# Eight key staging buffers, later scratch stores, new modelled costs and emission times, and another place for one FFN, in a two-layer decoder trunk on eight cores

## Chip, cores, metric

The kernel runs on the eight NeuronCores of one Trainium2 chip, one batch element on each. The metric is device microseconds of the slowest core. Cores 0 to 3 are one die, 4 to 7 the other. In some executions one die or both run at a lower granted clock and the time grows by some per cent; such runs are called slow, and only fast runs, or the cores of a die that was not disturbed, are compared here. On the chips of the experiments slow runs were frequent, so beside the ratios I give the *clean-die time*: for every die whose cores had a granted clock of 0.965 or more (median of its four cores), the span of its slowest core; of these values over all executions the median.

## The reference, cut

```python
D_MODEL, BATCH, SEQ, D_FF = 1024, 8, 4096, 2816
for i in range(2):                                 # layer 0: GLA, layer 1: differential attention
    x = x + 0.5 * swiglu_ffn(rms_norm(x, g), w_in, w_down)
    x = x + mixers[i](rms_norm(x, mix_norms[i]))
    x = x + 0.5 * swiglu_ffn(rms_norm(x, g2), w_in2, w_down2)
return rms_norm(x, final_norm)
# GLA: chunked gated linear attention, 4 heads, a state carried from chunk to chunk
# differential attention: 8 heads, causal; out = (softmax(Q1 K1') - lambda * softmax(Q2 K2')) V
```

## The kernel before

A core walks through its 4096 tokens in eight tiles of 512. For each tile `u` there are tasks: `gu0`/`down0` (first FFN), `gproj` (GLA projections), `core` (the sequential GLA chain), `gout`, `gu1`/`down1`, `gu2`/`down2` (two FFNs), `dproj` (Q, K, V of the differential attention), `att`, `dout`, `gu3`/`down3` (last FFN, final norm; it also stores the tile and loads the tokens of tile `u + 2`).

The program is a straight list of instructions for each engine, written by a small scheduler when the kernel is built. The scheduler keeps a *modelled* time of every engine and tile. It emits, of all pieces that are ready in modelled time, the one with the lowest key; each task has a range of keys from `v0` to `v1`. The modelled costs therefore do nothing on the chip except fix the order of instructions on each engine and queue. What is emitted early or late stays so in the list.

```python
    def _cost(self, eng, ins):                          # modelled duration, modelled latency
        ...                                             # PE: columns / 2400, + 0.1 for a row switch
            return c, 0.15
        if eng is self.act:
            return 0.2 + n * 0.0008, 0.1
        if eng is self.dve:
            return 0.15 + n * 0.00105, 0.1
        return (0.25 + n * 0.0012 if n > 16 else 0.3 + n * 0.1), 0.1
    def dma(self, q, dst, src, pairs, size=65536):
        ...
        self.dma_free = max(self.dma_free, at) + size / 235e3     # one modelled pipe for all queues
        done = max(at + 2.5, self.dma_free + 1.5)
```

Weights come in slots of up to 512 KB in a ring of twelve. On first use a slot is read as float32 and cast on the way by a DMA of the POOL queue (`wpack`; page of before: 160 of 512 KB, in the median 27.0 us from issue to landing), stored as bfloat16 to a scratch in HBM (`wscr`; 160, 12.4 us), and on later uses reloaded from there by the SP queue (1120, 4.4 us). A reload into a ring place must wait for the scratch store from that place; on core 3 the SP queue waited 185.4 us in all for scratch stores.

```python
    def acquire(sid):
        ...
        if t_scr[sid] is None:
            t_scr[sid] = Tl(f"scr{sid}", wst_sem[i])
            k.dma(SP, t_scr[sid], t_wring[i], [(wscr[sid, :, 0:ln], wring[i][:, 0:ln])], 256 * ln)
        return i
```

The keys of a tile are copied from PSUM by VectorE into one of two staging buffers and stored to HBM (`kvc`); the attention loads keys and values back in blocks.

```python
        def k_cons(c, b):                                # c: one of eight key chunks, b: its PSUM bank
            i = c % 2
            def chain():
                yield Need(DVE, rd=[t_bank[b]], wr=[t_kst[i]], cond=lambda: kdone[i])
                kdone[i] = False
                k.op(DVE, lambda: nc.vector.tensor_copy(out=kst[i][:], in_=bank[b][:]), ...)
                putbank(b)
                yield Need(SP, rd=[t_kst[i]])
                k.dma(SP, t_kc[c, t], t_kst[i], [(kvc[c, t, :, 0:512], kst[i][:])], 131072)
                kdone[i] = True
            spawn(chain())
```

The softmax here doesn't subtract the row's maximum and nothing guards it: scores larger than these inputs give would overflow.

## Time and profile before

| | before |
|---|---|
| time, median of 3 runs | 6155.62 us (6155.39 to 6157.76) |
| span of the profiled execution | 6197.9 us (core 6); core 3 6154.1 us |
| PE busy, VectorE, ScalarE | 92%, 41%, 34% |
| idle of PE in gaps over 0.8 us, core 3 | 363 us, 194 of them before 1000 us |

The gaps are mine: the start of each matmul record minus the start of the one before and its streaming time as the kernel's model has it (2400 columns per us, 4800 for matmuls of 64 rows; the trace of before, core 3, shows 512 columns every 0.216 us, and two 64-row matmuls of 256 columns, started 4 ns apart, every 0.110 us). The model's 0.1 us for a row switch is in keeping: at 5800.1 us four such 64-row matmuls take 0.32 us to the first start of the 128-row matmuls behind them, where two times 0.110 make 0.22. Where I name the task of a matmul, I matched the records one for one with the scheduler's list; cores 0 and 6 miss some records, so I read core 3. Core 6 also had one stretch of 160.8 us at a granted clock of 0.8125 (cores 0, 1 and 7 had one too), core 3 none; at that clock it costs about 30 of the 44 us between their spans, an estimate.

From the page of before, the engine line of PE (busy us, share of the span, instructions) and the line of the chain that ended last:

```profile
PE 5712.1 (92%) x36586; PEld 2907.6 (47%) x37216; DVE 2512.6 (41%) x4435; ACT 2120.1 (34%) x3826; POOL 530.9 (9%) x1070
...
PE 79%; DMA 9%; DVE 5%; issue 3%; ACT 2%; POOL 1%; SPq 1%; DVEq 0%; ACTq 0%; POOLq 0%
```

PE bounds the kernel; a gain comes from PE's idle time. The table of waits of before, core 6 (who waited for whom: us in total, times, longest). L1246 is the key copy, L732 and L880 are matmuls of the next tasks:

```profile
DVE sb_work L1246 <- DMA kvc<-sb_work: 137.6, 28, 37.3
...
PE ps_all L732 <- DVE sb_work L1246: 51.3, 7, 11.3
...
PE ps_all L880 <- DVE sb_work L1246: 44.4, 1, 44.4
```

The copy waits for the store of an older chunk, holds its PSUM bank meanwhile, and PE runs out of banks. I call such a wait of PE a stand. Two such places in the timeline of before, core 3, PE alone (start us, us, engine, line, operation, in brackets the idle time before and what ended it): the first key projection, and the seventh.

```profile
764.47 1.89 PE L880 MATMUL ps_all<-sb_wring,sb_hT 128*128 128x512 bf16 x8
810.65 1.87 PE L880 MATMUL ps_all<-sb_wring,sb_hT 128*128 128x512 bf16 x4 [44.28 <-DVE sb_work L1246]
...
4947.43 1.89 PE L732 MATMUL ps_all<-sb_hT,sb_wring 128*128 128x512 bf16 x8 [0.62 <-DVE sb_hT L629]
4959.84 2.72 PE L732 MATMUL ps_all<-sb_hT,sb_wring 128*128 128x512 bf16 x6 [10.53 <-DVE sb_work L1246]
```

The end of the kernel, core 3, cut into the stretch from `gout_7` to the start of attention 7, and attention 7 itself (busy time of each engine, granted clock, DMA share, GB/s):

```profile
5355.00:5722.00 367.00, 365.82 (x1830) 171.72 (x1830) 138.16 (x201) 67.60 (x133) 13.38 (x30) 1.00 0.49 154
5722.00:6001.00 279.00, 262.56 (x3134) 158.65 (x3134) 64.13 (x167) 245.95 (x324) 17.89 (x38) 0.99 0.54 153
```

In the first stretch PE is full; in the second it idles 16 us, and ScalarE (fourth busy time) is at 88%.

### The profile page before, as it was taken

The numbers are of one execution on the slowest core, as the hardware profiler recorded it, in microseconds if no ns is written. First come the engines' busy times: TensorE is split into PE (matmuls) and PEld (weight loads), VectorE is DVE, ScalarE is ACT, GpSimd is POOL, SyncE is SP. The second block draws the span as 40 slices with busy tenths as digits, with TensorE's granted clock in tenths as the row PEclk, the third lists the DMA queues.
The fourth block names the chain that finished last, engine by engine and source line by source line (L and its number), as shares of the span: only waits on it lengthen the run. The fifth ranks groups of instructions, "written<-read, shape, count | busy, mean of one in ns | idle before, by whom it ended". The sixth has DMA issues, their size and how long they took to land.

```text
span 6197.9 us, 103483 instructions; the slowest of 8 cores (6154.1 to 6197.9 us)
## 1 busy us (share of the span) xinstructions
PE 5712.1 (92%) x36586; PEld 2907.6 (47%) x37216; DVE 2512.6 (41%) x4435; ACT 2120.1 (34%) x3826; POOL 530.9 (9%) x1070
## 2 busy tenths in 40 slices
PE   5897759999999999999999999999999999899998
PEld 2443324444444454445544454445544445444554
DVE  3432155335633454334633345333453334443223
ACT  1211132124311452135411563115731157511791
POOL 1111111000100010010100001000010000100000
PEclk9998979999999999999999999998999999999999
DMA  9879967664345634465344753555534565345652
GB/s 217 200 172 210 207 145 183 189 195 147 123 139 168 185 129 140 149 188 155 126 141 149 202 151 120 157 165 160 151 120 142 170 181 158 91 159 147 172 152 99
DMA packets 331317, 984.58 MB, mean 159 GB/s; under 512 B 38447, under 2 KB 55232, under 8 KB 330816
## 3 DMA queue, kind: packets, MB, share of 16 engines
q1 hardware_dynamic: 306432, 891.88, 46.6%
q0 software_dynamic: 24384, 86.04, 9.5%
q8 instruction: 311, 5.10, 0.3%
q14 instruction: 190, 1.56, 0.1%
HBM read 944.11 MB, written 119.70 MB: 172 GB/s over the span
## 4 chain that ended last, share of the span: by engine, by line
PE 79%; DMA 9%; DVE 5%; issue 3%; ACT 2%; POOL 1%; SPq 1%; DVEq 0%; ACTq 0%; POOLq 0%
PE ps_all L732 36%; PE ps_all L807 17%; PE ps_all L1361 8%; PE ps_all L880 7%; PE ps_all L1326 4%; DMA sb_wring<-wpack 4%; PE ps_all L860 3%; DMA kvc<-sb_work 2%; PE ps_all L619 2%; DMA wscr<-sb_wring 2%; ACT sb_work L1331 1%; DMA sb_xt<-x 1%; DVE sb_hT L629 1%; DVE sb_work L1374 1%; SPq L222 1%
## 5 line engine op out<-in xcount | busy, mean ns | idle before, releaser
L732 PE MATMUL ps_all<-sb_hT,sb_wring 128*128 128x512 bf16 (+2 forms) x11344 | 2543.5, 376 | 110.7 <-DVE sb_work L1246 51.3
L732 PEld LDWEIGHTS ps_all<-sb_hT,sb_wring 128*128 128x128 bf16 x11648 | 1112.8, 99 | 1366.6 <-issue 192.7
L807 PE MATMUL ps_all<-sb_wring,sb_work 128*128 128x512 bf16 x5443 | 1289.4, 384 | 75.2 <-DMA sb_wring<-wpack 60.9
L1331 ACT ACTIVATE sb_work<-ps_all 128x1024 bf16<-128x1024 f32 (+1 forms) x1088 | 1019.5, 1000 | 389.8 <-PE ps_all L1326 387.3
L739 ACT ACTIVATE sb_th<-ps_all 128x512 f32<-128x512 f32 x704 | 420.2, 597 | 1923.1 <-PE ps_all L732 1913.8
L743 DVE SCALAR_TENSOR_TENSOR sb_tg<-sb_th,ps_all 128x512 f32<-128x512 f32 x704 | 483.4, 687 | 1147.8 <-ACT sb_th L739 1146.9
L807 PEld LDWEIGHTS ps_all<-sb_wring,sb_work 128*128 128x128 bf16 x5632 | 537.8, 98 | 693.7 <-issue 115.5
L880 PE MATMUL ps_all<-sb_wring,sb_hT 128*128 128x512 bf16 x2467 | 605.9, 387 | 79.3 <-DVE sb_work L1246 44.4
L600 ACT ACTIVATE sb_junk<-sb_xt 128x512 bf16<-128x512 f32 x448 | 282.0, 630 | 1082.0 <-DVE sb_xt L675 799.6
L1361 PE MATMUL ps_all<-sb_work 128*128 128x129 bf16 x8448 | 633.0, 222 | 12.5 <-DVE sb_work L1374 9.7
L751 DVE TENSOR_TENSOR sb_work<-ps_all,sb_tg 128x512 bf16<-128x512 f32 x704 | 486.4, 691 | 363.4 <-PE ps_all L732 317.5
L1361 PEld LDWEIGHTS ps_all<-sb_work 128*128 128x128 bf16 x8448 | 516.8, 98 | 195.6 <-issue 122.6
L675 DVE SCALAR_TENSOR_TENSOR sb_xt<-ps_all,sb_xt 128x512 f32<-128x512 f32 x256 | 172.7, 688 | 635.1 <-PE ps_all L807 616.9
L880 PEld LDWEIGHTS ps_all<-sb_wring,sb_hT 128*128 128x128 bf16 x2560 | 243.3, 99 | 349.8 <-issue 107.4
L1326 PE MATMUL ps_all<-sb_work 64*128 64x256 bf16 (+1 forms) x4352 | 356.5, 272 | 23.3 <-ACT sb_work L1331 18.3
L860 PE MATMUL ps_all<-sb_hT,sb_wring 128*128 128x512 bf16 x1492 | 349.1, 380 | 13.3 <-DVE sb_hT L629 7.4
L629 DVE TENSOR_TENSOR sb_hT<-ps_all,sb_norms 128x1024 bf16<-128x1024 bf16 x192 | 233.9, 1220 | 209.1 <-PE ps_all L619 198.2
L610 POOL TENSOR_SCALAR sb_ssq<-sb_ssq 128x1 f32<-128x1 f32 x224 | 87.0, 388 | 2685.6 <-ACT sb_junk L600 2685.0
L1326 PEld LDWEIGHTS ps_all<-sb_work 64*128 64x128 bf16 x4352 | 159.7, 95 | 227.0 <-issue 186.4
L860 PEld LDWEIGHTS ps_all<-sb_hT,sb_wring 128*128 128x128 bf16 x1536 | 146.6, 98 | 183.2 <-issue 21.4
L646 DVE TENSOR_SCALAR sb_hb<-sb_xt,sb_rstd 128x1024 bf16<-128x1024 f32 x192 | 143.9, 751 | 213.7 <-POOL sb_rstd L613 213.5
L619 PE MATMUL ps_all<-sb_ident,sb_hb 128*128 128x128 bf16 x1536 | 123.4, 227 | 80.2 <-DVE sb_hb L646 80.0
(87 smaller groups left out, 2478.6 us busy)
## 6 DMA issues: line engine op xcount, KB each, us to landing
sb_wring<-wscr SPq DMA_DIRECT2D x1120, 512.0 KB, 4.4
sb_work<-kvc SPq DMA_DIRECT2D x576, 258.0 KB, 3.0
sb_wring<-wpack POOLq DMA_DIRECT2D x160, 512.0 KB, 27.0
wscr<-sb_wring SPq DMA_DIRECT2D x160, 512.0 KB, 12.4
sb_xt<-x SPq DMA_DIRECT2D x32, 512.0 KB, 15.4
out<-sb_xt SPq DMA_DIRECT2D x32, 512.0 KB, 12.4
sb_wring<-wscr SPq DMA_DIRECT2D x56, 256.0 KB, 3.3
kvc<-sb_work SPq DMA_DIRECT2D x64, 130.0 KB, 15.0
```

The source lines that it names most:

```text
L600: k.op(ACT, lambda: nc.scalar.activation(out=junk[:], in_=xt[:, p, s, of * 512:(of + 1) * 512], func=AF.Square, accum_out=ssq[:, p, s, of: ...
L629: k.op(DVE, lambda: nc.vector.tensor_tensor(out=dst, in0=pt[:, :, :], in1=norms[:, n_idx, :].unsqueeze(2).to_broadcast([128, KC, 128]), op ...
L732: k.op(PE, lambda: nc.tensor.matmul(bank[b][:, lo:lo + n], lhsT=w[:, kc, u * 128:(u + 1) * 128], rhs=hT[:, p, kc, lo:lo + n], start=(kc == ...
L739: k.op(ACT, lambda: nc.scalar.activation(out=th[q][:], in_=bank[bg][:], func=AF.Tanh, scale=0.5), reads=[t_bank[bg]], writes=[t_th[q], t_b ...
L743: k.op(DVE, lambda: nc.vector.scalar_tensor_tensor(out=tg[r][:], in0=th[q][:], scalar=1.0, in1=bank[bg][:], op0=ALU.add, op1=ALU.mult), re ...
L751: k.op(DVE, lambda: nc.vector.tensor_tensor(out=act[:, c, :], in0=bank[bu][:], in1=tg[r][:], op=ALU.mult), reads=[t_tg[r], t_bank[bu]], wr ...
L807: k.op(PE, lambda: nc.tensor.matmul(bank[b][:], lhsT=act[:, c, s * 128:(s + 1) * 128], rhs=wring[i][:, (c % 4) * 512:(c % 4 + 1) * 512], s ...
L860: k.op(PE, lambda: nc.tensor.matmul(bank[b][:], lhsT=w[:, kc, cc * 128:(cc + 1) * 128], rhs=hT[:, p, kc, :], start=(kc == 0), stop=(kc == ...
L880: k.op(PE, lambda: nc.tensor.matmul(bank[b][:], lhsT=hT[:, p, kc, s * 128:(s + 1) * 128], rhs=wring[i][:, (kc % 4) * 512:(kc % 4 + 1) * 51 ...
L1326: k.op(PE, lambda: nc.tensor.matmul(psall[:, b0 + m, kk * 256:kk * 256 + w], lhsT=lhs, rhs=qT[m * 64:(m + 1) * 64, h, qs:qs + w], start=Tr ...
L1331: k.op(ACT, lambda: nc.scalar.activation(out=pT[pi][:, :, 0:ncol], in_=psall[:, b0:b0 + 2, 0:ncol], func=AF.Exp, scale=0.125), reads=[t_ba ...
L1361: k.op(PE, lambda: nc.tensor.matmul(obv[j][:, m, 0:129], lhsT=pT[pi][:, m, c0:c0 + 128], rhs=v, start=(it["first"] and kk == 0 and m == 0) ...
```

## The change

It means to take away the wait for the key staging, to bring the modelled durations nearer to the measured ones, to leave more work of the next tile for the end of each attention, and to give attention 7 (the last, with no next tile) tile 6's last FFN as company. Measured, core 3 of before, medians: a matmul of 512 columns took 0.38 us (its end as the profile models it) and ScalarE started 0.10 us later, 0.48 in all, modelled with its latency as 0.36 before and 0.46 after; ScalarE's squares took 0.63 us and the read of their sum 0.19, 0.82 together, modelled as 0.61 and 0.80; POOL's TENSOR_TENSOR of two columns took 0.71 us, modelled as 0.50 and 0.72; VectorE's operations on 512 columns took 0.69 us, modelled as 0.69 and 0.68. For the two DMA rates no measurement stands here: they are my estimates.

```diff
-        self.dma_free = 0.0
+        self.dma_free = {"sp": 0.0, "pool": 0.0}
...  # PE latency 0.15 -> 0.25; ACT, DVE, POOL latency 0.1 -> 0.2
-            return 0.2 + n * 0.0008, 0.1
+            return 0.2 + n * 0.0008 + (0.19 if len(ins.ins.outs) > 1 else 0.0), 0.2
-            return 0.15 + n * 0.00105, 0.1
-        return (0.25 + n * 0.0012 if n > 16 else 0.3 + n * 0.1), 0.1
+            return 0.22 + n * 0.0009, 0.2
+        if ins.ins.opcode == "TensorTensor":
+            return 0.41 + n * 0.157, 0.2
+        return 0.23 + n * 0.0012, 0.2
...
-        self.dma_free = max(self.dma_free, at) + size / 235e3
+        self.dma_free[q.name] = max(self.dma_free[q.name], at) + size / (180e3 if q.name == "pool" else 220e3)
...  # scratch store: no longer in acquire, but in a side chain, at the latest in release
+            keep[i] = sid
+            spawn(keeper(i, sid))
+    def keeper(i, sid):
+        yield Need(SP, rd=[t_wring[i]])
+        keep_now(i, sid)
...
-            i = c % 2                                    # key staging; value staging moves up by 6 KB
+            i = c                                        # eight buffers, kdone goes
...
-        v = (B + 0.0, B + 0.45, B + 0.7) if u != 1 else (-1.9, -1.7, -1.6)
+        v = (B + 0.0, B + 0.53, B + 0.79) if u != 1 else (-1.9, -1.7, -1.6)
...  # gproj: B + 0.7 to B + 1.06  ->  B + 0.79 to B + 1.14
-             ... B + 1.1, B + (3.2 if spare else 1.6), 76)              # gu3; spare: tile 6
+             ... B + (2.9 if spare else 1.1), B + (3.7 if spare else 1.6), 76)
-             B + (3.2 if spare else 1.6), B + (4.0 if spare else 2.6), 38)   # down3
+             B + (3.7 if spare else 1.6), B + (4.0 if spare else 2.6), 38)
```

More of the change, by code (lines that the diff above doesn't have):

```diff
@@ L164, in _cost @@
             eng.rows = rows
-            return c, 0.15
+            return c, 0.25
         if eng is self.act:
-            return 0.2 + n * 0.0008, 0.1
+            return 0.2 + n * 0.0008 + (0.19 if len(ins.ins.outs) > 1 else 0.0), 0.2
         if eng is self.dve:
-            return 0.15 + n * 0.00105, 0.1
-        return (0.25 + n * 0.0012 if n > 16 else 0.3 + n * 0.1), 0.1
+            return 0.22 + n * 0.0009, 0.2
+        if ins.ins.opcode == "TensorTensor":
+            return 0.41 + n * 0.157, 0.2
+        return 0.23 + n * 0.0012, 0.2
     def op(self, eng, fn, reads=(), writes=(), inc=True):
@@ L215, in dma @@
         q.free = at + 0.1 * len(pairs)
-        self.dma_free = max(self.dma_free, at) + size / 235e3
-        done = max(at + 2.5, self.dma_free + 1.5)
+        self.dma_free[q.name] = max(self.dma_free[q.name], at) + size / (180e3 if q.name == "pool" else 220e3)
+        done = max(at + 2.5, self.dma_free[q.name] + 1.5)
         for t in srcs:
@@ L442, in acquire, with keep_now @@
         if t_scr[sid] is None:
+            keep[i] = sid
+            spawn(keeper(i, sid))
+        return i
+    keep = {}
+    def keeper(i, sid):
+        yield Need(SP, rd=[t_wring[i]])
+        keep_now(i, sid)
+    def keep_now(i, sid):
+        if keep.get(i) == sid:
+            keep.pop(i)
             ln = slot_len(sid)
@@ L445, in acquire @@
             k.dma(SP, t_scr[sid], t_wring[i], [(wscr[sid, :, 0:ln], wring[i][:, 0:ln])], 256 * ln)
-        return i
     def release(i):
+        if i in keep:
+            keep_now(i, keep[i])
         rg["free"].append(i)
@@ L1189, in gla_core @@
         pool.update({4, 5})
-    kst_sem = [k.dsem(f"kst{i}") for i in range(2)]
+    kst_sem = [k.dsem(f"kst{i}") for i in range(8)]
     vst_sem = [[k.dsem(f"vst{i}_{h}") for h in range(4)] for i in range(2)]
@@ L1201, in diff_proj @@
         t_qT = [k.view(f"qT{h}", A_QT + h * TT * 2, A_QT + (h + 1) * TT * 2) for h in range(8)]
-        kst = [carve(R_ACT + i * 1024, 1024, BF16) for i in range(2)]
-        t_kst = [k.view(f"kst{i}", R_ACT + i * 1024, R_ACT + (i + 1) * 1024) for i in range(2)]
+        kst = [carve(R_ACT + i * 1024, 1024, BF16) for i in range(8)]
+        t_kst = [k.view(f"kst{i}", R_ACT + i * 1024, R_ACT + (i + 1) * 1024) for i in range(8)]
         VB = 4 * 4 * 130 * 2
-        vo = R_ACT + 2048
+        vo = R_ACT + 8192
         vst = [carve(vo + i * VB, VB, BF16, "p (h s c) -> p h s c", h=4, s=4) for i in range(2)]
@@ L1211, in diff_proj @@
         vleft = [NS, NS]
-        kdone = [True, True]
         def v_cons(hf, s, b):
@@ L1240, in k_cons @@
         def k_cons(c, b):
-            i = c % 2
+            i = c
             def chain():
-                yield Need(DVE, rd=[t_bank[b]], wr=[t_kst[i]], cond=lambda: kdone[i])
-                kdone[i] = False
+                yield Need(DVE, rd=[t_bank[b]], wr=[t_kst[i]])
                 k.op(DVE, lambda: nc.vector.tensor_copy(out=kst[i][:], in_=bank[b][:]),
@@ L1251, in chain @@
                 k.dma(SP, t_kc[c, t], t_kst[i], [(kvc[c, t, :, 0:512], kst[i][:])], 131072)
-                kdone[i] = True
             spawn(chain())
@@ L1460, in _build @@
         task(f"gproj_{u}", lambda u=u: gla_proj(u), [f"~down0_{u}"]
-             + ([f"dproj_{u - 1}"] if u else []), B + 0.7, B + 1.06, 43)
+             + ([f"dproj_{u - 1}"] if u else []), B + 0.79, B + 1.14, 43)
         task(f"core_{u}", lambda u=u: gla_core(u), [f"gproj_{u}"] + ([f"att_{u - 1}"] if u else []), -500.0, -500.0, 1)
@@ L1478, in _build @@
         task(f"gu3_{t}", lambda t=t, g=spare: ffn_gu(t, 3, G_E if g else A_KV),
-             [f"~dout_{t}", f"att_{t}"] + ([f"core_{t + 1}"] if spare else []), B + 1.1, B + (3.2 if spare else 1.6), 76)
+             [f"~dout_{t}", f"att_{t}"] + ([f"core_{t + 1}"] if spare else []), B + (2.9 if spare else 1.1), B + (3.7 if spare else 1.6), 76)
         task(f"down3_{t}", lambda t=t, g=spare: ffn_down(t, 3, final_block(t), not g), [f"~gu3_{t}"],
-             B + (3.2 if spare else 1.6), B + (4.0 if spare else 2.6), 38)
+             B + (3.7 if spare else 1.6), B + (4.0 if spare else 2.6), 38)
     for t in range(min(2, NTL)):
```

## The prediction

> **What bounds the kernel now.** TensorE: the page's engine table has PE busy 5712 of 6198 us (92%), VectorE 41%, ScalarE 34%; the chain that ended last is PE for 79%, DMA for 9%. A gain must come from time in which PE idles or runs at half clock. On core 3 (6154 us in the table of cores) the gaps over 0.8 us between matmul records sum to 363 us, 194 of them before 1000 us. From 372 to 744 us the slices show the DMA engines full (about 1.03); the change moves no fewer bytes, so this stays.
>
> **Eight key staging buffers.** With two, the copy of key chunk 2 waits until chunk 0's store landed, and holds its PSUM bank. The table of waits: VectorE at the key copy waits 137.6 us in 28 waits for the store; PE waits 51.3 + 44.4 us for the copy. On core 3 PE stands 44.5 us at 766 us, then 4.8, 4.9, 7.1, 9.8, 8.8 and 10.7 us after the next six key projections: about 90. A half-clock stretch (granted 0.5) follows each and outlasts the gap, costing about 2 us each. [...] In the last six places nearly all should come back: stores will be issued during the query projection, and landing takes 10 to 15 us here. At 766 us the SP queue is also held by slot stores and reloads (one per 5.5 us up to 802 us), so I count 30 of 44. Together 90 us.
>
> **Scratch stores as the slot lands.** Slightly later, in the same queue: about 0.
>
> **Recalibrated costs and times.** PE waits for transposes whose inputs are late: about 5 us in most cores of the linear attention, 1 to 3 us around it, 2.8 us in each key projection, because the order assumed shorter latencies. Longer ones put filler there, and the later emission times leave some 17 instead of 7 us of the next tile's projection for each attention's end. These places idle about 125 us; I count 42, because tile 7's core has little filler.
>
> **FFN of tile 6 beside attention 7.** Its 75 us of gate and up matmuls all ran before 5723 us, in a full stage. Attention 7 takes 286 us with 37 us of filler. Its steps take 0.915 us on PE (QK, PV, two row switches) against 0.904 us per exponential on ScalarE (timeline): both nearly full; filler adds its own length. Only the waits over 0.2 us, about 20 us with clock loss, are recovered: 12 us.
>
> **Sum.** 90 + 42 + 12 = 144 us, less 14 for new waits of a new order: 130 us.
>
> Predicted 6025 us, range 5975 to 6095. Chances: faster by over 2% (below 6032.5) 0.55, within 2% 0.43, slower 0.02.
>
> **Right if** PE's wait for the key copy falls under 10 us; the 766 us gap shrinks by over 25; the 5 us gap goes in most cores; attention 7's stage grows to about 330 us while the stage before shrinks by about 65; the slices from 372 to 744 us stay.
>
> **Wrong if** key stores land so late that the next FFN's activation writes, which reuse the staging space, or attention's key loads wait; the new order exposes waits where tile 6's FFN was filler; or the startup's DMA order shifts.

The sum came to 90 + 42 + 12 - 14 = 130 us.

## The result, and the profile after

| | before | after |
|---|---|---|
| median | 6155.51 us (6153.78 to 6157.76, 4 runs) | 6078.63 us (fast runs 6072.95 to 6081.79; one slow run 7032.02) |
| ratio of fast runs | | 0.9872, 95% interval 0.9852 to 0.9891 |
| idle of PE in gaps over 0.8 us, core 3 | 363 us (169 after 1000 us) | 271 us (109 after 1000 us) |
| PE busy | 92% | 95% |

A ratio is the mean time of one kernel's fast runs over that of the other's of the same rounds, so not quite the ratio of the medians quoted beside it. The gain is 77 us by the medians; I had predicted 130, with 6095 us as the upper end. The 77 us are probably low: in the profiled run of after, the cores of die 0 had some 30 stretches of at most 8 us at a granted clock of 0.8125 (170 us in all on core 3), those of die 1 none, and in all three fast runs die 1 was done sooner (slowest core 6057 to 6064 us, die 0 6072 to 6081). Against die 1 the gain is 91 us or more.

From the page of after, the same two lines:

```profile
PE 5741.2 (95%) x37536; PEld 2917.1 (48%) x37536; DVE 2509.4 (41%) x4435; ACT 2119.3 (35%) x3826; POOL 525.9 (9%) x1070
...
PE 85%; DMA 7%; DVE 3%; issue 2%; ACT 2%; POOL 1%; SPq 1%; DVEq 0%; POOLq 0%; ACTq 0%
```

The table of waits of after, core 2. The key copy is L1260 here; L1339 is the attention's QK matmul:

```profile
DVE sb_work L1260 <- PE ps_all L876: 128.3, 64, 10.0
...
PE ps_all L1339 <- DMA sb_work<-kvc: 23.0, 2, 21.5
```

The copy now waits for PE alone, and PE for the copy not at all. But PE waits 23 us for the first load of keys and values. The same two places as before, timeline of after, core 3, PE:

```profile
788.47 0.58 PE L977 MATMUL ps_all<-sb_wg2b,sb_work 17*128 17x512 bf16 x1 [9.62 <-ACT sb_work L1014]
809.03 0.50 PE L1339 MATMUL ps_all<-sb_work 64*128 64x256 bf16 x4 [19.98 <-DMA sb_work<-kvc]
...
4872.13 1.89 PE L876 MATMUL ps_all<-sb_hT,sb_wring 128*128 128x512 bf16 x8
4878.32 1.01 PE L635 MATMUL ps_all<-sb_ident,sb_hb 128*128 128x128 bf16 x8 [4.30 <-DVE sb_hb L662]
```

Both stands have been replaced by another. At the first place, 44 us became 9.6 and 20 us. Before the 9.6 us, ScalarE's exponentials of the linear attention (L1012, L1014) waited 11.5 us for a key store to land: their output `Eb` lies over the eight staging buffers. At the seventh projection, 10.5 us became 4.3 us, and this new stand, a wait for the transposes (L635) of the next tokens' norm, is there after all six later projections with the same length; in the kernel before these transposes never caused more than 1.8 us there. Its cause is on ScalarE: timeline of after, core 3, ACT. L1249 are the copies of the query chunks, L616 the squares of the new tokens' norm:

```profile
4871.94 0.59 ACT L1249 CAST sb_work<-ps_all 128x512 bf16<-128x512 f32 x1 [1.14 <-PE ps_all L876]
4874.11 0.59 ACT L1249 CAST sb_work<-ps_all 128x512 bf16<-128x512 f32 x1 [1.59 <-PE ps_all L876]
4874.59 0.64 ACT L616 ACTIVATE sb_junk<-sb_xt 128x512 bf16<-128x512 f32 x1
```

The squares of the last token block stand in the list behind the last query copy, and they started behind it, at 4874.59 us, when the projection was over (its last matmul ended at 4874.02 us). The tokens were not late: at the projection before this one (core 3), the load of the last block landed at 4088.6 us, and its squares started at 4099.8 us, 11 us later and 0.5 us after the start of the last query copy (4099.32 us).

The end of the kernel, core 3, in the same two stretches as before:

```profile
5283.00:5594.00 311.00, 310.85 (x1580) 146.97 (x1578) 117.88 (x171) 58.52 (x119) 13.38 (x30) 1.00 0.50 155
5594.00:5910.00 316.00, 311.58 (x3390) 177.60 (x3390) 84.62 (x197) 257.66 (x340) 17.64 (x38) 1.00 0.55 162
```

56 us left the first stretch, 37 came back in the second, whose idle time on PE fell from 16 to 4 us.

### The profile page after: what moved, and what is told of

Read it like the earlier page. It is cut to its first block, busy times and chain, and to the rows that moved or that the text cites. A ratio compares the mean times of both kernels' runs of the same rounds, so it can differ in the third digit from the quotient of the medians.

```text
span 6071.9 us, 104625 instructions; the slowest of 8 cores (6050.0 to 6071.9 us)
## 1 busy us (share of the span) xinstructions
PE 5741.2 (95%) x37536; PEld 2917.1 (48%) x37536; DVE 2509.4 (41%) x4435; ACT 2119.3 (35%) x3826; POOL 525.9 (9%) x1070
## 4 chain that ended last, share of the span: by engine, by line
PE 85%; DMA 7%; DVE 3%; issue 2%; ACT 2%; POOL 1%; SPq 1%; DVEq 0%; POOLq 0%; ACTq 0%
PE ps_all L748 37%; PE ps_all L823 18%; PE ps_all L1374 8%; PE ps_all L896 8%; PE ps_all L876 5%; PE ps_all L1339 5%; DMA sb_wring<-wpack 4%; DMA wscr<-sb_wring 3%; PE ps_all L635 2%; ACT sb_work L1344 1%; SPq L224 1%; DVE sb_hT L645 0%; POOL sb_ssq L626 0%; POOL sb_rstd L629 0%; DVE sb_work L1387 0%
## 5 line engine op out<-in xcount | busy, mean ns | idle before, releaser
L748 PE MATMUL ps_all<-sb_hT,sb_wring 128*128 128x512 bf16 (+2 forms) x11968 | 2570.4, 371 | 26.3 <-DVE sb_hT L645 10.9
L748 PEld LDWEIGHTS ps_all<-sb_hT,sb_wring 128*128 128x128 bf16 x11968 | 1133.3, 99 | 1284.4 <-issue 127.3
L823 PE MATMUL ps_all<-sb_wring,sb_work 128*128 128x512 bf16 x5632 | 1310.4, 385 | 53.2 <-DMA sb_wring<-wpack 53.1
L616 ACT ACTIVATE sb_junk<-sb_xt 128x512 bf16<-128x512 f32 x448 | 282.1, 630 | 1044.2 <-DVE sb_xt L691 783.4
L1374 PE MATMUL ps_all<-sb_work 128*128 128x129 bf16 x8448 | 617.6, 222 | 19.5 <-DVE sb_work L1387 17.0
L896 PE MATMUL ps_all<-sb_wring,sb_hT 128*128 128x512 bf16 x2560 | 618.4, 387 | 18.6 <-DVE sb_hT L645 12.2
L1374 PEld LDWEIGHTS ps_all<-sb_work 128*128 128x128 bf16 x8448 | 500.4, 98 | 173.0 <-issue 142.9
L1339 PE MATMUL ps_all<-sb_work 64*128 64x256 bf16 (+1 forms) x4352 | 359.2, 272 | 46.1 <-DMA sb_work<-kvc 23.0
L1339 PEld LDWEIGHTS ps_all<-sb_work 64*128 64x128 bf16 x4352 | 156.9, 95 | 259.2 <-issue 222.2
L876 PEld LDWEIGHTS ps_all<-sb_hT,sb_wring 128*128 128x128 bf16 x1536 | 149.8, 99 | 177.8 <-issue 23.1
L635 PE MATMUL ps_all<-sb_ident,sb_hb 128*128 128x128 bf16 x1536 | 122.0, 225 | 89.3 <-DVE sb_hb L662 89.2
```

What stands on the lines that cost most here:

```text
L616: k.op(ACT, lambda: nc.scalar.activation(out=junk[:], in_=xt[:, p, s, of * 512:(of + 1) * 512], func=AF.Square, accum_out=ssq[:, p, s, of: ...
L635: k.op(PE, lambda: nc.tensor.transpose(pt[:, kc, :], src_fn(kc), ident[:]), reads=[t_src, t_ident], writes=[t_bank[b]], inc=(kc == KC - 1))
L748: k.op(PE, lambda: nc.tensor.matmul(bank[b][:, lo:lo + n], lhsT=w[:, kc, u * 128:(u + 1) * 128], rhs=hT[:, p, kc, lo:lo + n], start=(kc == ...
L823: k.op(PE, lambda: nc.tensor.matmul(bank[b][:], lhsT=act[:, c, s * 128:(s + 1) * 128], rhs=wring[i][:, (c % 4) * 512:(c % 4 + 1) * 512], s ...
L876: k.op(PE, lambda: nc.tensor.matmul(bank[b][:], lhsT=w[:, kc, cc * 128:(cc + 1) * 128], rhs=hT[:, p, kc, :], start=(kc == 0), stop=(kc == ...
L896: k.op(PE, lambda: nc.tensor.matmul(bank[b][:], lhsT=hT[:, p, kc, s * 128:(s + 1) * 128], rhs=wring[i][:, (kc % 4) * 512:(kc % 4 + 1) * 51 ...
```

## Experiments

Two theories at the start. Theory 1 is the prediction's: the staging buffers are the largest part and the parts add up. Theory 2, from the trace after: behind each key staging wait stands a second one that the new order made or left, so the buffers are worth little in the whole, and the gain comes from the order. All twelve kernels gave correct results. The first four ran on one chip, the second four on another, the last four on a third.

| run | clean-die time us | kernel before, same chip | difference |
|---|---|---|---|
| e1_staging | 6112.9 | 6168.5 | -56 |
| e2_costs | 6122.5 | 6168.5 | -46 |
| e3_times | 6133.4 | 6168.5 | -35 |
| e4_tile6 | 6154.2 | 6168.5 | -14 |
| f1_after_again | 6075.4 | 6170.4 | -95 |
| f2_sp_rate | 6022.8 | 6170.4 | -148 |
| f3_pool_stores | 6065.8 | 6170.4 | -105 |
| f4_two_staging | 6070.9 | 6170.4 | -100 |
| g1_two_rate235 | 6055.3 | 6183.9 | -129 |
| g2_rate_pool | 6010.5 | 6183.9 | -173 |
| g3_rate260_pool | 6045.1 | 6183.9 | -139 |
| g4_keeper | 6197.2 | 6183.9 | +13 |

On the third chip the kernel before itself spread from 6152 to 6233 us on clean dies, so its differences are rough.

### e1_staging: the staging buffers alone

```diff
 # the kernel before with
-            i = c % 2
+            i = c
```

> The kernel before with the eight key staging buffers alone (their copies, stores and the room they take), everything else as before. Theory 1, as predicted: about 90 us faster, ratio 0.985, the stand at 766 us shrinks by 30 us or more and the six stands after the later key projections (46 us on core 3) go. Theory 2, from the trace after: at 766 us the wait only moves to attention 0's first key load, which stands in the SP queue behind ten slot stores that are awaited one by one, so under 10 us comes back there; the six later places give about 40 to 60 us: ratio 0.991 to 0.993. Rival 3: the stores were never the limit and the gain came from the order: ratio over 0.997.

Ratio 0.9890 (0.9846 to 0.9934), two fast runs of eight. Theory 1's 90 us did not come. On core 5 of the undisturbed die, set against core 3 of before, the stretch from the end of the first key projection to `gu3_0` is 10 us shorter (165.5 against 175.4 us; I had predicted 30), and the rest of the gain lies around the six later projections. Rival 3, no gain from the buffers, is out: alone they are worth some 56 us.

### e2_costs: the modelled costs alone, two staging buffers

```diff
 # the kernel before with the hunks of _cost and of dma_free, nothing else
```

> The kernel before with the recalibrated costs alone (engine costs and the two DMA rates), with the old emission times and two staging buffers. Theory 1: this brings most of what the order gives, 20 to 40 us. Theory 2: the gaps between an attention and the next gate-and-up stage of tiles 1 to 4 (about 9 us of idle PE each, plus clock) shrink only in part, because the projection is used up before attention ends; the longer modelled latencies use filler faster and cost some 5 to 10 us in attentions 5 and 6: 0 to 20 us in all, ratio 0.997 to 1.0.

Ratio 0.9913 (0.9884 to 0.9943): 46 us, more than both theories said. The waits, core 3 of this run (the key copy is L1248, L734 and L862 are matmuls):

```profile
DVE sb_work L1248 <- DMA kvc<-sb_work: 91.8, 27, 25.5
...
PE ps_all L862 <- DVE sb_work L1248: 14.0, 2, 13.3
...
PE ps_all L734 <- DVE sb_work L1248: 0.5, 1, 0.5
```

With the same two buffers VectorE still waits for the stores, but PE waits for the copies 14.5 us instead of some 91 (45.9, 44.3 and 1.1 us on core 3 of before). That is less than it seems, because most of the wait only bears another name. At the first place PE stands 13.3 us for a copy, then 22.0 us for an operation of VectorE (L930) that stands in VectorE's list right behind the last key copy, then 6.8 us for a load of keys and values: 42 us, against 44. VectorE and PE there, core 3 of e2:

```profile
803.05 0.69 DVE L1248 CAST sb_work<-ps_all 128x512 bf16<-128x512 f32 x1 [6.56 <-DMA kvc<-sb_work]
...
804.20 0.61 DVE L930 SCALAR_TENSOR_TENSOR sb_tg<-sb_th,ps_all 128x512 f32<-128x512 f32 x1
...
804.96 10.15 PE L882 MATMUL ps_all<-sb_wring,sb_hT 128*128 128x512 bf16 x36 [21.97 <-DVE sb_tg L930]
```

After each of the six later projections stands a wait of 3.48 us for the transposes of the next tokens' norm, the one that the kernel after has. Counting all waits there (table under g1), the order alone takes away 15 of 54 us. Where the rest of the 46 us comes from was not tested. I expected 0 to 20 us because I looked for the effect in the attentions only.

### e3_times: the emission times alone

```diff
-        v = (B + 0.0, B + 0.45, B + 0.7) if u != 1 else (-1.9, -1.7, -1.6)
+        v = (B + 0.0, B + 0.53, B + 0.79) if u != 1 else (-1.9, -1.7, -1.6)
 # and gproj B + 0.79 to B + 1.14
```

> The kernel before with the later emission times of the next tile's first FFN and projection alone. Both theories: the leftover of the projection (about 17 instead of 7 us) fills PE after attentions 1 to 4; if this is what closed the gaps there in the kernel after, it gives 30 to 50 us alone (ratio about 0.993) and those gaps (9 us each on core 3) fall under 2 us. If it needs the longer latencies too, it gives under 15 us.

Ratio 0.9929 (0.9894 to 0.9964): 35 us, as expected where the times alone close the gaps after attentions 1 to 4. The traces agree (core 3): PE's waits in the 45 us after the ends of attentions 2, 3 and 4 fall from 7.7, 7.9 and 9.0 us before to 0, 0 and 1.7 us; e2, with the costs alone, leaves 6.5, 6.5 and 10.2. The waits of about 5 us in the linear attention's cores of tiles 2 to 5 go here too, and stay in e2 (4.6 to 5.6 us).

### e4_tile6: tile 6's FFN alone

```diff
-             ... B + 1.1, B + (3.2 if spare else 1.6), 76)
+             ... B + (2.9 if spare else 1.1), B + (3.7 if spare else 1.6), 76)
 # and down3 from B + 3.7
```

> The kernel before with only the FFN of tile 6 moved beside attention 7. Theory 1, as predicted: 12 us faster (ratio 0.998), attention 7 with its filler 320 to 335 us instead of 286, the stage before it about 65 us shorter. Rival, if attention 7 were bound by ScalarE: attention 7 grows by under 20 us and 50 us or more are gained. From the trace after (642 us for the two stages before, 623 after) I expect 15 to 20 us.

Ratio 0.9966 (0.9938 to 0.9994): 14 us. The predicted 12 us hold, and the rival, 50 us or more, is out: in its trace (core 3) attention 7 takes 310.5 us instead of 279.7, so it is nearly as full on PE as on ScalarE.

The four parts give 151 us alone. The change as a whole gives 77 in the first measurement, with die 0 disturbed, and 95 in the next one.

### f1_after_again: the yardstick

No edit.

> The kernel after, unchanged, as the yardstick for the three other runs on this chip. First measurement: ratio 0.987. The four parts alone gave, on undisturbed dies, about 61 (staging), 50 (costs), 36 (times) and 17 us (tile 6), 164 in sum; both theories say that the whole gives far less than the sum, 75 to 105 us (ratio 0.983 to 0.988).

95 us on clean dies, only two fast runs of the kernel before, so no ratio. The whole is 56 us less than the sum of its parts.

### f2_sp_rate: one number of the model

```diff
-        ... size / (180e3 if q.name == "pool" else 220e3)
+        ... size / (180e3 if q.name == "pool" else 235e3)
```

> The kernel after with one number changed: the modelled rate of the SP queue 235 instead of 220 KB per us. This moves the squares of the last new token block before the last three query copies on ScalarE at the end of each differential projection. Theory A: the 4.5 us stand at the end of each of six projections in the kernel after comes from that order, and eats what the staging buffers gave there; so the stands fall under 1.5 us and the kernel is 20 to 40 us faster than f1. Rival B: the DMA queues are full there and the stand is another wait for data; then they stay, or a wait of the same length comes at attention's first key load, and the time is within 8 us of f1.

6022.8 against 6075.4 us of f1 on the same chip: 53 us faster, more than theory A's 20 to 40, with one fast run of five (6023.57 us; f1's fast runs 6077 to 6088). Timeline of f2, core 4, seventh projection, ACT, where L1249 and L616 are as in the kernel after:

```profile
4835.99 0.63 ACT L616 ACTIVATE sb_junk<-sb_xt 128x512 bf16<-128x512 f32 x1
...
4837.43 0.57 ACT L1249 CAST sb_work<-ps_all 128x512 bf16<-128x512 f32 x1
4838.96 0.59 ACT L1249 CAST sb_work<-ps_all 128x512 bf16<-128x512 f32 x1 [0.96 <-PE ps_all L876]
4840.69 0.59 ACT L1249 CAST sb_work<-ps_all 128x512 bf16<-128x512 f32 x1 [1.14 <-PE ps_all L876]
```

And PE at the same place:

```profile
4831.80 8.80 PE L876 MATMUL ps_all<-sb_hT,sb_wring 128*128 128x512 bf16 x40
4840.43 0.61 PE L635 MATMUL ps_all<-sb_ident,sb_hb 128*128 128x128 bf16 x8
4840.88 9.31 PE L748 MATMUL ps_all<-sb_hT,sb_wring 128*128 128x384 bf16 x74
```

The squares now stand three query copies ahead of the end, and PE goes from the projection to the transposes and the next FFN without a stand. Rival B falls: there was no other wait of that length behind it. Added up by stretches (medians of the cores with complete records), about 25 of the 52 us between f1 and f2 lie at the ends of the six projections; the rest is spread over the attentions with their first FFNs, and I did not take it apart.

### f3_pool_stores: the first place

```diff
+            q, sm = (POOL, wpl_sem) if sid >= W_DIFF else (SP, wst_sem)
+            t_scr[sid] = Tl(f"scr{sid}", sm[i])
+            k.dma(q, t_scr[sid], ...)
```

> The kernel after with the scratch stores of the differential projection's twelve input slots and four output slots (first tile only) on the POOL queue instead of the SP queue. Theory A: near 790 us attention 0's first key load waits in the SP queue behind stores and reloads that wait for one another, about 5 us for each of ten slots; without them the stand of 20 us there falls under 8 us and the kernel is 15 to 30 us faster than f1. Rival B: DMA bandwidth or the landing of the key stores sets that time; then the stand moves by under 5 us.

10 us against f1, less than theory A's 15 to 30. In the kernel after, core 3, the SP queue goes like this before attention 0 (stores, then reloads that wait for them, the key and value loads last):

```profile
788.21 0.38 SPq L224 DMA_DIRECT2D wscr<-sb_wring  x1
793.30 0.32 SPq L224 DMA_DIRECT2D sb_wring<-wscr  x1
793.71 0.38 SPq L224 DMA_DIRECT2D wscr<-sb_wring  x1
...
804.96 2.57 SPq L224 DMA_DIRECT2D sb_work<-kvc  x5
```

In f3, core 4, SP queue:

```profile
764.27 5.43 SPq L224 DMA_DIRECT2D sb_wring<-wscr  x4
769.91 9.41 SPq L224 DMA_DIRECT2D sb_work<-kvc  x5
```

And PE in f3, core 4, at the start of attention 0 (L1341 is its QK matmul there):

```profile
806.61 0.51 PE L1341 MATMUL ps_all<-sb_work 64*128 64x256 bf16 x4 [10.75 <-DMA sb_work<-kvc]
```

The loads are issued 35 us earlier, and the first of them lands at 806.5 us all the same, 36.6 us after its issue, against a median of 3.1 us for the same load (258 KB) over the whole kernel after: it was issued behind four slot reloads, of 512 KB each, while the DMA engines were full or nearly so (share 1.09 from 750 to 780 us, 0.86 from 780 to 810). Here the landings keep the order of issue: the four reloads land at 787.1, 792.8, 798.8 and 803.0 us, the load at 806.5. The landing came only 2.4 us earlier than in the kernel after (808.9 us there). So both theories were half right: the stand fell from 20 to 10.8 us, and in what is left PE waits for a load that was issued long before and lands behind the reloads.

### f4_two_staging: two buffers in the changed kernel

```diff
 # the kernel after with the staging hunks undone
-            i = c
+            i = c % 2
```

> The kernel after with two key staging buffers instead of eight. Theory A (the staging gain at the six later projections is mostly eaten in the kernel after by the late squares): only 15 to 30 us slower than f1, much less than the 61 us that staging gives alone. Rival B (the parts add up): about 60 us slower than f1.

6070.9 us on three clean dies (one fast run, 6073.28 us), against 6075.4 us with eight buffers. In the kernel after, the eight buffers are worth nothing that these runs can see: even less than theory A said.

### g1_two_rate235: two buffers with the better rate

```diff
 # f4 with
-            ... else 220e3)
+            ... else 235e3)
```

> The kernel after with the SP rate of 235 in the model (as in f2) and two key staging buffers instead of eight. f4 showed that with the rate of 220 the eight buffers are worth nothing (undisturbed cores 6047 to 6072 us with two, 6055 to 6087 with eight). Theory A: they were worth nothing because the late squares of the last token block end the same stretch anyway; with the squares early the buffers count again, so this is 30 to 50 us slower than f2 (cores near 6050 to 6065 us). Rival C: the recalibrated order alone already plans around two buffers, and the 50 us of f2 come from the order whatever the buffers; then the cores are near 6015 to 6030 us.

6055.3 us, cores of its one fast run 6037.5 to 6055.3, on another chip than f2 (6003.0 to 6022.5 us, its fast run) but the same as g2, which has eight buffers and the pool stores: 6010.5 us, 45 us less. Of these some 10 us are the pool stores' (f3 against f1), so the buffers are worth about 35 us here, an estimate from these two differences. Theory A holds: with the late squares gone the buffers count again. The trace of its fast run shows it. On core 3 the key copies end PE's waits again, as here after the fourth projection:

```profile
2661.15 7.15 PE L748 MATMUL ps_all<-sb_hT,sb_wring 128*128 128x384 bf16 x64
2673.76 6.42 PE L748 MATMUL ps_all<-sb_hT,sb_wring 128*128 128x512 bf16 x21 [5.46 <-DVE sb_work L1262]
```

Sums of PE's waits over 0.3 us around the ends of the six later projections (12 us before to 20 us after the last matmul of the projection; core 3, of e1 core 5, of f2 core 4; before, e1 and e2 have the old emission times):

| | two buffers | eight buffers |
|---|---|---|
| old costs | before 53.8 | e1 2.8 |
| new costs, rate 220 | e2 38.6 | after 25.8 |
| new costs, rate 235 | g1 26.9 | f2 4.4 |

At rate 220 the buffers take away 13 us there, at 235 22, with the old costs 51. What cancels even the 13 us in f4 against f1 stays open, as f4 has no fast profile.

### g2_rate_pool, g3_rate260_pool: both mends, and a rate of 260

```diff
 # g2: the edits of f2 and of f3 together; g3: the same with
+            ... else 260e3)
```

> The kernel after with both mends: SP rate 235 in the model (f2, cores 6003 to 6022 us, about 50 under f1) and the differential slots' scratch stores on the POOL queue (f3, about 12 under f1). They touch different places, so the parts should add: cores near 5995 to 6010 us, ratio to the kernel before 0.973 to 0.976, which beats both kernels by more than 2% against before. If the pool stores' gain was chance, it equals f2.

> As g2, with the modelled SP rate 260. This puts the squares of the last token block seven instead of three query copies ahead of the projection's end. If the squares' place is the whole of f2's gain, nothing more comes: within 10 us of g2. If there was more time in modelled landings that are too late, another 10 to 30 us.

g2: ratio 0.9693 (0.9582 to 0.9803), two fast runs, 6011.84 and 6012.32 us; clean dies 6010.5. By the ratio and by the clean dies (2.8%) it beats the kernel before by more than 2%, but the interval reaches 0.9803, so the 2% are not certain; the kernel after had 6073 to 6088 us in its fast runs on two other chips. g3: ratio 0.9748 (0.9637 to 0.9859), clean dies 6045.1 us. Modelling the queue still faster does not help; whether it costs the 35 us between them is not sure, because in g3 several cores had a lower granted clock (0.973 on cores 0 and 1 of its profiled run, which took 6061 and 6062 us, against 0.981 on cores 4 to 7, which took 5998 to 6012 us).

### g4_keeper: the later scratch stores alone

> The kernel before with the scratch stores issued by a waiting side chain instead of at the acquisition, nothing else. PE, ScalarE, VectorE and POOL have the same instructions in the same order as before; only the SP queue's order differs. All theories: no gain, cores within 15 us of the kernel before.

One fast run, 6214.17 us, on clean dies 6181.7 and 6212.8 us, where the kernel before had 6152 to 6233 us on that chip. No gain. Its instructions on PE, ScalarE, VectorE and POOL are the same in the same order as before.

## Why the prediction was right or wrong

- **The time.** 130 us predicted, 77 measured, 6078.63 us inside the range but near its upper end; the ratio 0.9872 makes it less than 2% faster, the second likeliest of the three classes I gave. That the time fell inside the range was in part luck: the largest term came out as nothing and the next one at about double, and the two errors partly cancel.
- **The term that was mis-sized**: "Together 90 us" for the eight staging buffers. Alone they gave 56 us (e1); in the kernel after they gave nothing (f4 against f1). Two steps under it failed. The first is "so I count 30 of 44": from the end of the first key projection to `gu3_0`, core 3, before and after differ by only 2 us (175.4 and 173.4), because other waits took over: 9.6 us behind ScalarE's writes over the staging space, which the prediction had named under "Wrong if" (for an FFN's writes; here they are the linear attention's), and 20 us for attention 0's first loads, which waited for their turn in the SP queue (issued at 804.96 us), and in f3, where they are issued at 769.91 us, landed behind four reloads while the DMA share was 1.09 and then 0.86. The second is "In the last six places nearly all should come back". The key copies stopped waiting as I said, yet a stand of 4.3 us came in place of each: it waits for the squares of the next tokens, placed behind the query copies by a modelled queue rate of 220 KB per us. f2 moved them with one number; the stands went, and the kernel was 53 us faster, about half of it at these places. I had named "the new order exposes waits" as a danger, and tied it to tile 6 only.
- **Recalibrated costs and times, "I count 42"**: too small. The kernel without the eight buffers (f4) is 100 us faster than before, 14 of them from tile 6, so the order gives some 85. The mechanism was in part another: the 5 us waits of the linear attention, which I laid to the assumed latencies, stay with the new costs (e2) and go with the later emission times (e3). The buffers and the order do not add, though I added them: the new costs bring the late squares, which end the same stretches as the key copies.
- **Tile 6, 12 us**: right (14 alone; in the whole, 56 us leave the stretch before attention 7 and 37 come back). So was the mechanism: 0.915 us on PE against 0.904 us on ScalarE for each step means that filler adds nearly its own length.
- **Scratch stores, about 0**: no run contradicts it (g4).
- **The slices from 372 to 744 us stay**: they did; the DMA share there is 1.03 in each slice of core 3, before and after. The gap sums before 1000 us fell only from 194 to 162 us.
- **The clock.** Half-clock stretches (granted 0.5) come with the stands in the kernel after as before: on core 3 one of 3.4 or 6.8 us at each of the six stands of 4.3 us. In all they sum there to 314 us before and 273 after. At the seven stands of before they outlast the gap by 2.8 to 5.4 us, which fits the 2 us each; the first is 44.4 us long, the other six 3.4 to 10.2. That part of the argument was not tested by itself.

## What to carry to other kernels

When a list scheduler fixes each engine's order, a modelled rate is a tuning knob like any other: one DMA rate, 220 instead of 235, put a small ScalarE operation behind work it did not depend on, and cost about 50 us in all, half of it traced to that operation. A wait that leaves the table of waits is not always gone: in e2 it came back under the name of the next operation in the same list. Before adding buffers for a wait, ask what PE would do next if the wait were gone, and follow that piece back through every list it stands in. Parts that remove the same idle time do not add; measure each alone and each taken away.
